# Modulation rows of a hybrid decoder layer: sums in two stages, products with ones at the stages' ends

## The chip, the cores and the metric

The kernel runs on one core of a Trainium2 chip. Times are device microseconds (us) of the whole program on that core. The profile shows one execution, with times counted from the start of its span.

## What is computed

One decoder layer for 1024 tokens of width 1024: a normalized and modulated input goes through one projection into four mixers (a forgetting attention, a chunked spatial gating, a Mamba-2 state space model, an mLSTM), whose outputs are normalized, joined and projected back; then a mixture of 32 experts, and a last norm. What the change touches is the modulation by the condition `c`:

```
cond = silu(c)
mod = cond @ w_ada + b_ada
shift1, scale1, gate1, shift2, scale2, gate2 = split(mod, 6)
h = rms_norm(x) * (1 + scale1) + shift1
x = x + gate1 * hybrid_mixer(h, ...)
h = rms_norm(x) * (1 + scale2) + shift2
x = x + gate2 * hierarchical_moe(h, ...)
```

`shift1` and `scale1` are made early. The other four rows of 1024 values (gate1, shift2, scale2 with the norm's gain folded in, gate2) are wanted only after the mixers, and go to a small table `mod_d` in device memory, one row each.

## The kernel before, in words

The program is a chain of stages, each written as a Python function. Data are tiles of 128 partitions. The mixers' input is held as a high and a low part (`hH`, `hL`), and so is each piece of weights (`wh`, `wl`): `load_w` loads `wraw` by SP (line 134; a second range by ACT), ACT writes the high part (line 53), DVE the low one (line 61), and every projection is three matmuls (hH wh, hH wl, hL wh) for each of eight slices of the inner dimension, in a PSUM bank named `ps`. Small products go to banks named `pq`.

Around the change the stages are, in the order of the program:

- the mLSTM's projections LQ, LK (channel-major, 128x512 matmuls), LV and LO (token-major: eight tiles of 24 matmuls of 128x256 each). ACT evicts them as `qT`, `kT`, `va` and, with a sigmoid, `so`. The eight `so` tiles are stored to `so_d` by SP (line 591) and loaded again as `ym` (line 658) when the outputs are made.
- the mLSTM's recurrence over eight chunks of 128 tokens (lines 597 to 649), then for each pair of chunks a head norm, the product with `ym` and a store to `y_tok` by SP (lines 650 to 660, 494).
- `ssd_inputs`: three pieces of projection; ACT evicts every bank twice, as `craw` and scaled as `xbc`; DVE adds the other three taps of a convolution, ACT applies SiLU. Then the state space model (`ssd`) and its output (`ssd_out`).
- `spatial_gating`: its weights `sgw` and gain `sgg` are loaded by ACT (lines 759, 765); eight tiles of `sgv`, two head norms, and eight tiles in which `ug` (ACT, two buffers) is multiplied into `sgy` (DVE, lines 782, 784), which SP stores.
- `attention_proj` (lines 791 to 823): 192 matmuls that give `q` and `k`, evicted by ACT and DVE; then the attention.

`modulation` (lines 546 to 565) is called ahead of the mLSTM. For each of the four rows it loads eight tiles `mw` of 512 KB by SP (three buffers), multiplies each by a column of `cond` and adds them up on DVE in `macc` (one buffer). Then ACT loads the row of `b_ada` into `mr` (one buffer), two matmuls of 512 columns with a column of ones sum `macc` over the partitions, DVE adds them to `mr`, and ACT stores the row to `mod_d`:

```
mr = mp.tile([1, 2, D], F32, name="mr", bufs=1)
nc.scalar.dma_start(mr[:, 0, :], b_ada[:, cs])
for c in (slice(0, 512), slice(512, D)):
    o = pq1()
    mm(o[0:1], ones[:, 0:1], acc[:, c], True, True)
    nc.vector.tensor_add(mr[:, 0, c], mr[:, 0, c], o[0:1])
nc.scalar.dma_start(mod_d[i:i + 1], mr[:, 0])
```

The order of each engine's instructions is not that of the text. A scheduler of the tile framework places them when the program is built, by its own estimate of when each could start; after that every engine, and every DMA queue (SP's, ACT's, POOL's), goes through its list in order. Tiles live in pools that open and close; a pool that opens in the memory of a closed one waits for the last instruction or transfer that used it.

Of the kernel before, what the change touches and what calls it, by code (L numbers as in the profile page):

```python
# [9 lines left out]
F32 = mybir.dt.float32  # L10
# [9 lines left out]
P = 128  # L20
S = 1024
D = 1024
# [14 lines left out]
def hybrid_block_kernel(ctx, tc, x, c, w_in, w_out, w_mix_norm, attn_f_bias, sg_w, sg_b,  # L37
# [4 lines left out]
    nc = tc.nc  # L42
# [12 lines left out]
    def mm(o, l, r, start, stop):  # L55
        return nc.tensor.matmul(o, l, r, start=start, stop=stop)  # L56
# [6 lines left out]
    def pool(stack, name, side, bufs=1):  # L63
        return stack.enter_context(tc.tile_pool(name=name, bufs=bufs, side=side))
# [7 lines left out]
    ones = consts.tile([P, P], F32, name="ones")  # L72
# [108 lines left out]
    with tc.tile_pool(name="st", bufs=1, side="left") as st, tc.tile_pool(name="stx", bufs=6, side="left") as stx, \  # L181
# [5 lines left out]
        xts, was, accs = {}, {}, {}  # L187
# [60 lines left out]
        for i in range(2):  # L248
            o = 0
# [29 lines left out]
        for g, (k0, k1) in enumerate(GS):  # L279
# [6 lines left out]
            acc = accs[g]  # L286
            o = pq1()
# [29 lines left out]
        for t in range(NT):  # L317
            o = os[t]
# [222 lines left out]

    tab_d = dram.tile([S * NE, 4], F32, name="tab_d")

    def modulation(mp):
        for i in range(4):
            cs = slice((2 + i) * D, (3 + i) * D)
            acc = mp.tile([P, D], F32, name="macc", bufs=1)
            for k in range(KT):
                wt = mp.tile([P, D], F32, name="mw", bufs=3)
                nc.sync.dma_start(wt, w_ada[k * P:(k + 1) * P, cs])  # L550
                if k == 0:
                    nc.vector.tensor_scalar(acc, wt, cond[:, k:k + 1], None, op0=OP.mult)
                else:
                    nc.vector.scalar_tensor_tensor(acc, wt, cond[:, k:k + 1], acc, op0=OP.mult, op1=OP.add)
            mr = mp.tile([1, 2, D], F32, name="mr", bufs=1)
            nc.scalar.dma_start(mr[:, 0, :], b_ada[:, cs])
            if i == 2:
                nc.scalar.dma_start(mr[:, 1, :], w_norm2)
            for c in (slice(0, 512), slice(512, D)):
                o = pq1()  # L560
                mm(o[0:1], ones[:, 0:1], acc[:, c], True, True)
                nc.vector.tensor_add(mr[:, 0, c], mr[:, 0, c], o[0:1])
            if i == 2:
                nc.vector.scalar_tensor_tensor(mr[:, 0], mr[:, 0], 1.0, mr[:, 1], op0=OP.add, op1=OP.mult)
            nc.scalar.dma_start(mod_d[i:i + 1], mr[:, 0])


    def mlstm(ml, wk):
# [17 lines left out]
        so_d = dram.tile([S, GW], F32, name="so_d")  # L586
        w = load_w((LO, LO + GW))
        for t in range(NT):
            so = wk.tile([P, GW], F32, name="so", tag="ym")
            act(so, tok_major(w, t)[:, :GW], AF.Sigmoid)  # L590
            nc.sync.dma_start(so_d[t * P:(t + 1) * P], so)

        C = [ml.tile([P, 2, 2 * VW], F32, name=f"C{i}") for i in range(2)]
        for i in range(2):
# [149 lines left out]
    def ssd_out(y, wk):  # L744
        w = load_w((MZ, MZ + GW))
        for t in range(NT):
            z = wk.tile([P, GW], F32, name="z")
            act(z, tok_major(w, t)[:, :GW], AF.Silu)
            nc.vector.tensor_mul(y[:, t, :], y[:, t, :], z)
        for t0 in (0, 4):  # L750
            yv = y[:, t0:t0 + 4, :].rearrange("p t (h d) -> p t h d", d=DH)
            head_norm(wk, yv, yv, 4)
            y_out(y[:, t0:t0 + 4, :], 2, t0, 4)
# [189 lines left out]
    ml = pool(m1, "ml", "right")  # L943
    mlw = pool(m1, "mlw", "right", 2)
    m2 = ExitStack()
    modulation(pool(m2, "mp", "right"))
    mlstm(ml, mlw)
    m2.close()
    m3 = ExitStack()
    xbc = ssd_inputs(pool(m3, "sA", "left"))  # L950
    m1.close()
    sB = pool(m3, "sB", "left", 2)
    y_ssd = ssd(xbc, sB)
    with ExitStack() as m4:
        ssd_out(y_ssd, sB)
        spatial_gating(pool(m4, "sgp", "right"))
    m3.close()
    with ExitStack() as m4:
        attention_proj(pool(ph1, "qp", "left"), pool(m4, "augp", "right"))
    proj.close()  # L960
# [176 lines left out]
    with ExitStack() as m4:  # L1137
# [263 lines left out]
        with tc.manual_schedule():  # L1401
# [15 lines left out]
            for t in range(NT):  # L1417
# [4 lines left out]
                o = ps1()  # L1422
                mixed(t, 0, o, 0, 4)
                if last:
                    x1T, f = turned(t - 1)
# [12 lines left out]
                if not last:  # L1438
# [3 lines left out]
                    f = [half(i) for i in range(2)]  # L1442
# [13 lines left out]
                o = ps1()  # L1456
# [761 lines left out]
```

## Time and profile before

| | us |
|---|---|
| median of 3 runs (lowest, highest) | 1273.74 (1273.19, 1274.29) |
| profiled execution | 1273.05 |
| its span | 1271.3 |
| mean granted clock of TensorE in it | 0.966 |
| PE busy | 1153.3 (91%) |
| DVE busy | 801.5 (63%) |
| ACT busy | 589.3 (46%) |
| POOL busy | 326.3 (26%) |

The profiled execution lies 1.75 us above its span, which counts from the first to the last instruction. In a timeline a row is one instruction (or several of a kind in a row, with their number): its start, its length, the engine, the source line, what it writes and reads; in brackets stand the idle time of the engine ahead of it and what ended it. A line 53, 56 or 61 is that of a helper, so the tiles' names tell which instruction it is. Issues of transfers on a queue carry a q behind the engine's name, and their length is that of the issue alone. A record of PE is longer than the distance to the next one, because matmuls are pipelined. The granted clock is a share of 2.4 GHz; 0.50 is 1.2 GHz.

### The profile page before, as it was taken

The page shows a single profiled execution, that of the slowest core. Times are in us where ns is not written, and L with a number is a line of the kernel's source. Part 1 is how long each engine was busy: PE and PEld are TensorE (multiplying, and loading weights), DVE is VectorE, ACT ScalarE, POOL GpSimd, SP SyncE. Part 2 cuts the span into 40 slices and gives each one's busy share as a digit, 9 for nine tenths or more (in the row PEclk, how much of TensorE's full clock was granted, in tenths as well). Part 3 has the DMA queues.
Part 4 walks back from the last instruction along what each step waited for, and adds up shares of the span by engine and source line. Part 5 has one row for each costly group of instructions (what it writes and reads, how often), then busy time and mean ns, then how long its engine had stood idle before and what let it go on. Part 6 is the DMA issues. An engine that isn't in the chain of part 4 may idle for free. (4 is left out here: it accounts for less than half of the span.)

```text
span 1271.3 us, 18583 instructions
## 1 busy us (share of the span) xinstructions
PE 1153.3 (91%) x6455; PEld 868.1 (68%) x6455; DVE 801.5 (63%) x1460; ACT 589.3 (46%) x909; POOL 326.3 (26%) x314
## 2 busy tenths in 40 slices
PE   4689879999999899999959999999999999999981
PEld 3577667879998788787747754466676557665660
DVE  6976667757643488488878941335654564555674
ACT  6442114354743488344437841224553443554563
POOL 2420000002102277333321942102322132222111
PEclk8699999999999999999969999999999999999996
DMA  9614884222221123675477999999999998999975
GB/s 268 203 32 149 261 271 118 89 71 53 73 60 34 42 65 111 203 267 199 162 296 290 328 332 377 376 403 372 385 378 378 357 389 317 341 367 384 337 274 198
DMA packets 96452, 305.48 MB, mean 240 GB/s; under 512 B 15106, under 2 KB 53756, under 8 KB 71772
## 3 DMA queue, kind: packets, MB, share of 16 engines
q1 hardware_dynamic: 84762, 284.47, 60.9%
q0 software_dynamic: 8464, 17.13, 5.8%
q10 hardware_dynamic: 3122, 2.56, 0.6%
q8 instruction: 57, 0.93, 0.3%
q14 instruction: 47, 0.39, 0.1%
HBM read 283.86 MB, written 32.06 MB: 249 GB/s over the span
## 5 line engine op out<-in xcount | busy, mean ns | idle before, releaser
L1649 POOL DMA_INDIRECT x_d<-yt,tabi x34 | 62.1, 1827 | 240.7 <-DVE yt L1623 186.7
L56 PE MATMUL ps<-wu,xTs 128*64 128x512 f32 x256 | 119.5, 599 | 1.8 <-DMA wu<-in_w_expert_up_dram 1.8
L56 PE MATMUL ps<-wg,xTs 128*64 128x512 f32 x256 | 119.8, 599 | 0.0
L56 PE MATMUL ps<-wh,hH 128*128 128x256 f32 (+1 forms) x336 | 96.9, 289 | 8.2 <-ACT so L53 4.9
L56 PE MATMUL ps<-wl,hH 128*128 128x256 f32 (+1 forms) x336 | 95.8, 286 | 0.0
L56 PE MATMUL ps<-wh,hL 128*128 128x256 f32 (+1 forms) x336 | 95.2, 288 | 0.0
L56 PE MATMUL ps<-hH,wh 128*128 128x512 f32 x224 | 89.1, 398 | 0.5 <-ACT xbc L53 0.4
L56 PE MATMUL ps<-hH,wl 128*128 128x512 f32 x224 | 89.4, 399 | 0.0
L56 PE MATMUL ps<-hL,wh 128*128 128x512 f32 x224 | 89.0, 397 | 0.0
L56 PEld LDWEIGHTS ps<-wh,hH 128*128 128x128 f32 x336 | 64.4, 192 | 11.4 <-ACT so L53 5.5
L56 PE MATMUL ps<-split,xTH 128*128 128x512 f32 x200 | 69.4, 403 | 1.0
L56 PEld LDWEIGHTS ps<-wg,xTs 128*64 128x64 f32 x256 | 32.1, 136 | 54.6 <-issue 51.3
L1640 POOL TENSOR_TENSOR yt<-yt,g2bc 128x1024 f32<-128x1024 f32 x14 | 33.7, 2409 | 137.5 <-ACT yt L53 121.4
L53 ACT ACT_TABLE_LOAD x47 | 60.3, 1283 | 17.7 <-DVE xbc L680 5.9
L53 ACT ACTIVATE xTH<-pq 128x512 fp32r<-128x512 f32 x33 | 18.4, 592 | 100.9 <-PE pq L1664 100.9
L56 PE MATMUL ps<-wh,xTH 128*128 128x512 f32 (+1 forms) x156 | 63.8, 409 | 1.4 <-PEq L1869 0.5
L56 PEld LDWEIGHTS ps<-wl,hH 128*128 128x128 f32 x336 | 64.1, 191 | 0.9 <-issue 0.9
L61 DVE TENSOR_TENSOR wl<-wu,wh 128x1024 fp32r<-128x1024 f32 x39 | 47.2, 1222 | 27.4 <-ACT wh L53 26.7
L56 PEld LDWEIGHTS ps<-wh,hL 128*128 128x128 f32 x336 | 64.3, 194 | 0.0
L56 PE MATMUL ps<-wl,xTH 128*128 128x512 f32 (+1 forms) x156 | 61.3, 393 | 0.5 <-DVE wl L61 0.5
L56 PE MATMUL pq<-wd,aTs 128*64 128x512 f32 x256 | 58.7, 597 | 3.0 <-PEq L1857 2.1
L53 ACT ACTIVATE sg<-ps 128x512 f32<-128x512 f32 (+1 forms) x32 | 18.9, 592 | 91.1 <-PE ps L56 49.8
(550 smaller groups left out, 3241.2 us busy)
## 6 DMA issues: line engine op xcount, KB each, us to landing
wg<-in_w_expert_gate_dram SPq DMA_DIRECT2D x64, 1024.0 KB, 9.5
wu<-in_w_expert_up_dram SPq DMA_DIRECT2D x64, 1024.0 KB, 8.1
wd<-in_w_expert_down_dram SPq DMA_DIRECT2D x64, 1024.0 KB, 7.5
mw<-in_w_ada_dram SPq DMA_DIRECT2D x32, 512.0 KB, 5.0
wraw<-in_w_in_dram SPq DMA_DIRECT2D x20, 512.0 KB, 3.6
xt<-in_x_dram SPq DMA_DIRECT2D x16, 512.0 KB, 4.1
wt<-in_w_ada_dram SPq DMA_DIRECT2D x16, 512.0 KB, 5.4
woraw<-in_w_out_dram SPq DMA_DIRECT2D x16, 256.0 KB, 3.4
```

The lines of the kernel that those rows point to most:

```text
L53: return nc.scalar.activation(o, i, f, **kw)
L56: return nc.tensor.matmul(o, l, r, start=start, stop=stop)
L61: (eng or nc.vector).tensor_sub(lo, src, hi.bitcast(F32))
L1640: nc.gpsimd.tensor_mul(yt[:, on_dve * 512:], yt[:, on_dve * 512:], g2bc[:, on_dve * 512:])
L1649: nc.gpsimd.indirect_dma_start(out=x1_d, out_offset=bass.IndirectOffsetOnAxis(ap=tok, axis=0), in_=yt, in_offset=None, bounds_check=S - 1, ...
```

## The change

`modulation` takes the rows `js` that it is to sum, keeps one `macc` tile for each, and returns a function that does the rest for these rows: `b_ada`'s load, the two products, the adds and the store. The rows 0 and 1 are summed beside the mLSTM's projections, and their products are written behind `mlstm`; the rows 2 and 3 are summed beside the gating, and their products are written behind `spatial_gating`. The `so_d` stores move from SP's queue to ACT's. `ssd_out` and the closing of its pools move ahead of the gating's pools. What is computed stays the same.

```diff
--- before.py
+++ after.py
@@ -541,10 +541,11 @@
 
     tab_d = dram.tile([S * NE, 4], F32, name="tab_d")
 
-    def modulation(mp):
-        for i in range(4):
+    def modulation(mp, js):
+
+        accs = {i: mp.tile([P, D], F32, name=f"macc{i}", bufs=1) for i in js}
+        for i, acc in accs.items():
             cs = slice((2 + i) * D, (3 + i) * D)
-            acc = mp.tile([P, D], F32, name="macc", bufs=1)
             for k in range(KT):
                 wt = mp.tile([P, D], F32, name="mw", bufs=3)
                 nc.sync.dma_start(wt, w_ada[k * P:(k + 1) * P, cs])
@@ -552,17 +553,26 @@
                     nc.vector.tensor_scalar(acc, wt, cond[:, k:k + 1], None, op0=OP.mult)
                 else:
                     nc.vector.scalar_tensor_tensor(acc, wt, cond[:, k:k + 1], acc, op0=OP.mult, op1=OP.add)
+
+        def rows_of(i):
+            cs = slice((2 + i) * D, (3 + i) * D)
             mr = mp.tile([1, 2, D], F32, name="mr", bufs=1)
             nc.scalar.dma_start(mr[:, 0, :], b_ada[:, cs])
             if i == 2:
                 nc.scalar.dma_start(mr[:, 1, :], w_norm2)
             for c in (slice(0, 512), slice(512, D)):
                 o = pq1()
-                mm(o[0:1], ones[:, 0:1], acc[:, c], True, True)
+                mm(o[0:1], ones[:, 0:1], accs[i][:, c], True, True)
                 nc.vector.tensor_add(mr[:, 0, c], mr[:, 0, c], o[0:1])
             if i == 2:
                 nc.vector.scalar_tensor_tensor(mr[:, 0], mr[:, 0], 1.0, mr[:, 1], op0=OP.add, op1=OP.mult)
             nc.scalar.dma_start(mod_d[i:i + 1], mr[:, 0])
+
+        def mod_rows():
+            for i in js:
+                rows_of(i)
+
+        return mod_rows
 
 
     def mlstm(ml, wk):
@@ -588,7 +598,7 @@
         for t in range(NT):
             so = wk.tile([P, GW], F32, name="so", tag="ym")
             act(so, tok_major(w, t)[:, :GW], AF.Sigmoid)
-            nc.sync.dma_start(so_d[t * P:(t + 1) * P], so)
+            nc.scalar.dma_start(so_d[t * P:(t + 1) * P], so)
 
         C = [ml.tile([P, 2, 2 * VW], F32, name=f"C{i}") for i in range(2)]
         for i in range(2):
@@ -943,18 +953,22 @@
     ml = pool(m1, "ml", "right")
     mlw = pool(m1, "mlw", "right", 2)
     m2 = ExitStack()
-    modulation(pool(m2, "mp", "right"))
+    mod_rows = modulation(pool(m2, "mp", "right"), (0, 1))
     mlstm(ml, mlw)
+    mod_rows()
     m2.close()
     m3 = ExitStack()
     xbc = ssd_inputs(pool(m3, "sA", "left"))
     m1.close()
     sB = pool(m3, "sB", "left", 2)
     y_ssd = ssd(xbc, sB)
+    ssd_out(y_ssd, sB)
+    m3.close()
     with ExitStack() as m4:
-        ssd_out(y_ssd, sB)
-        spatial_gating(pool(m4, "sgp", "right"))
-    m3.close()
+        sgp = pool(m4, "sgp", "right")
+        mod_rows = modulation(pool(m4, "mp", "right"), (2, 3))
+        spatial_gating(sgp)
+        mod_rows()
     with ExitStack() as m4:
         attention_proj(pool(ph1, "qp", "left"), pool(m4, "augp", "right"))
     proj.close()
```

What the scheduler makes of it, at three places. In the lists a row is a line of the program, an instruction and its tiles; xN stands for N in a row.

SP's queue beside the projections, before; `mw` are the sums' weights, `wraw` the projections' weights (the first here is LO's), `rb` rows that the recurrence reads:

```order
L550 DMA mw<-in_w_ada_dram 128x1024 x11
L134 DMA wraw<-in_w_in_dram 128x4x256
L550 DMA mw<-in_w_ada_dram 128x1024 x3
L134 DMA wraw<-in_w_in_dram 128x4x256
L550 DMA mw<-in_w_ada_dram 128x1024 x3
L599 DMA rb<-nrow_d 128x4x128
L550 DMA mw<-in_w_ada_dram 128x1024 x2
L599 DMA rb<-nrow_d 128x4x128
```

and after the change:

```order
L551 DMA mw<-in_w_ada_dram 128x1024 x16
L134 DMA wraw<-in_w_in_dram 128x4x256
L609 DMA rb<-nrow_d 128x4x128 x2
L134 DMA wraw<-in_w_in_dram 128x4x256
L609 DMA rb<-nrow_d 128x4x128 x2
L134 DMA wraw<-in_w_in_dram 128x4x256 x3
L668 DMA ym<-so_d 128x2x256
L134 DMA wraw<-in_w_in_dram 128x4x256
```

All 16 `mw` of the first two rows now stand ahead of LO's weights, where 11 of the 32 stood.

ACT at the end of the recurrence, before (`kt` and `ex` belong to the recurrence's last chunks, `hnq` and `hnv` to the head norms, `craw` and `xbc` are the first evictions of `ssd_inputs`):

```order
L53 ACTIVATE ex<-ex 128x512
L53 ACTIVATE hnq<-num 128x512
L53 ACTIVATE craw<-ps_2089 128x512
L53 ACTIVATE xbc_2085<-ps_2089,cols 128x512
L53 ACTIVATE kt<-pq_1882 128x256
L53 ACTIVATE kt<-pq_1925 128x256
L53 ACTIVATE ex<-ex 128x512
L53 ACTIVATE kt<-pq_1968 128x256
L53 ACTIVATE ex<-ex 128x512
L53 ACTIVATE hnq<-num 128x512
L53 ACT_TABLE_LOAD
```

and after the change, from the last `hnq` on:

```order
L53 ACTIVATE hnq<-num 128x512
L569 DMA mod_d<-mr 1x1024
L560 DMA mr<-in_b_ada_dram 1x1024
L53 ACTIVATE hnv<-hnv 128x8
L769 DMA sgw<-in_sg_w_dram 128x4x128
L569 DMA mod_d<-mr 1x1024
L775 DMA sgg<-in_w_mix_norm_dram 128x256
L53 ACTIVATE craw<-ps_2019 128x512
L53 ACTIVATE xbc_2015<-ps_2019,cols 128x512
L53 ACTIVATE craw<-ps_2046 128x512
L53 ACTIVATE xbc_2015<-ps_2046,cols 128x509
```

The two stores to `mod_d`, the load of `b_ada` between them and `sgw` now stand ahead of the first `craw` and `xbc`, which before stood between two `kt` of the recurrence. On PE the four products of rows 0 and 1 stand right behind the recurrence's last `va,ex`, three matmuls ahead of the end of a bank.

ACT at the end of the gating, before (`ug` are the gating's evictions, `q_0` and `k_0` the first of attention_proj):

```order
L53 ACTIVATE ug<-ps_3517 128x256
L53 ACTIVATE ug<-ps_3553 128x256
L53 ACTIVATE wh<-wraw 128x4x256
L134 DMA wraw<-in_w_in_dram 128x4x128
L53 ACTIVATE wh<-wraw 128x4x256
L53 ACTIVATE q_0_3609<-ps_3633 64x512
L53 ACTIVATE q_0_3610<-ps_3633 64x512
L53 ACTIVATE q_1_3621<-ps_3633 64x512
```

and after the change:

```order
L53 ACTIVATE ug<-ps_3538 128x256
L53 ACTIVATE wh<-wraw 128x4x256
L134 DMA wraw<-in_w_in_dram 128x4x128
L53 ACTIVATE wh<-wraw 128x4x256
L569 DMA mod_d<-mr 1x1024
L560 DMA mr<-in_b_ada_dram 1x1024
L569 DMA mod_d<-mr 1x1024
L53 ACTIVATE q_0_3613<-ps_3637 64x512
```

The stores of rows 2 and 3 and a load stand ahead of `q_0` and `k_0`. On PE the four products of rows 2 and 3 stand behind the gating's last `sgv,wT`, and the attention's first logits, which stood behind all 192 matmuls of attention_proj, stand behind its first 48.

## Rows read from the trace of the kernel before

**Rows 1.** The page, part 1: busy time (share) and instructions of each engine.

```profile
PE 1153.3 (91%) x6455; PEld 868.1 (68%) x6455; DVE 801.5 (63%) x1460; ACT 589.3 (46%) x909; POOL 326.3 (26%) x314
```

**Rows 2.** Busy time by stretch (us, instructions), granted clock, DMA share, GB/s.

```profile
160.00:200.00 40.00, 31.53 (x233) 27.14 (x234) 23.07 (x31) 7.39 (x14) 0.00 (x0) 1.00 0.67 227
200.00:250.00 50.00, 49.62 (x337) 40.15 (x338) 43.43 (x126) 24.53 (x41) 3.12 (x5) 1.00 0.34 96
...
350.00:400.00 50.00, 50.00 (x389) 48.26 (x389) 20.05 (x30) 17.39 (x28) 1.90 (x2) 1.00 0.20 56
```

**Rows 3.** Waits of PE, 100 to 200 us: total us, times, longest.

```profile
PE ps L56 <- ACT so L53: 4.9, 3, 3.0
PE pq L56 <- DVE macc L554: 4.5, 2, 2.9
...
PE ps L56 <- ACT va L53: 0.7, 1, 0.7
```

**Rows 4.** Timeline of PE beside the projections: start, length, instruction, idle time before it.

```profile
128.94 0.39 PE L56 MATMUL ps<-hH,wh 128*128 128x512 f32 x1
129.17 0.40 PE L56 MATMUL ps<-hH,wl 128*128 128x512 f32 x1
131.96 3.27 PE L56 MATMUL pq<-macc,ones 128*1 128x512 f32 x4 [2.39 <-issue]
...
137.12 0.28 PE L56 MATMUL ps<-wh,hH 128*128 128x256 f32 x1
137.24 0.28 PE L56 MATMUL ps<-wl,hH 128*128 128x256 f32 x1
...
171.43 1.88 PE L56 MATMUL pq<-macc,ones 128*1 128x512 f32 x4 [2.94 <-DVE macc L554]
...
199.88 0.72 PE L56 MATMUL pq<-qT,kT 64*128 64x128 f32 x8
```

**Rows 5.** Timeline of SP's DMA issues, 110 to 250 us.

```profile
112.06 20.15 SPq L550 DMA_DIRECT2D mw<-in_w_ada_dram  x11
132.26 0.43 SPq L134 DMA_DIRECT2D wraw<-in_w_in_dram  x1
...
239.96 0.36 SPq L658 DMA_DIRECT2D ym<-so_d  x1
```

**Rows 6.** Groups of DVE instructions, 110 to 200 us: busy and mean, idle before.

```profile
L554 DVE SCALAR_TENSOR_TENSOR macc<-mw,cond,macc 128x1024 f32<-128x1024 f32 x28 | 36.4, 1301 | 13.2 <-DMA mw<-in_w_ada_dram 12.8
...
L562 DVE TENSOR_TENSOR mr<-mr,pq 1x512 f32<-1x512 f32 x8 | 5.4, 674 | 5.4 <-PE pq L56 5.4
...
L671 DVE MEMSET craw<- 128x3 f32 x1 | 0.1, 61 | 1.3 <-DMA mod_d<-mr 1.3
```

**Rows 7.** Timeline of ACT, 112 to 400 us.

```profile
138.88 1.06 ACT L53 ACTIVATE wh<-wraw 128x1024 fp32r<-128x1024 f32 x1 [0.96 <-DMA wraw<-in_w_in_dram]
...
154.27 0.22 ACTq L565 DMA_DIRECT2D mod_d<-mr  x1
...
160.48 0.22 ACTq L556 DMA_DIRECT2D mr<-in_b_ada_dram  x1
...
219.13 0.58 ACT L53 ACTIVATE craw<-ps 128x512 f32<-128x512 f32 x1
...
396.75 1.06 ACT L53 ACTIVATE wh<-wraw 128x1024 fp32r<-128x1024 f32 x1 [5.38 <-DMA wraw<-in_w_in_dram]
```

**Rows 8.** Timeline of PE: end of the recurrence, and of the gating.

```profile
233.96 0.47 PE L56 MATMUL ps<-hH,wh 128*128 128x512 f32 x1
...
390.65 0.48 PE L56 MATMUL ps<-hH,wh 128*128 128x512 f32 x1
```

**Rows 9.** DMA issues, 108 to 200 us: KB each, median us to landing.

```profile
ym<-so_d SPq DMA_DIRECT2D x1, 256.0 KB, 2.8
```

**Rows 10.** Busy time by stretch (as rows 2), first logits of the attention.

```profile
440.00:445.00 5.00, 4.21 (x20) 3.63 (x20) 2.46 (x7) 2.72 (x9) 4.18 (x4) 0.50 0.15 57
```

**Rows 11.** Timeline of DVE, 250 to 256 us.

```profile
253.81 0.35 DVE L700 SCALAR_TENSOR_TENSOR ex<-rb,cum,mneg 128x128 f32<-128x128 f32 x1 [2.74 <-DMA rb<-arow_d]
```

## The prediction

> **What bounds the kernel now.** I read the page's totals first, then the busy time by stretch, then the waits of PE, then the timelines of PE, ACT, DVE and SP around the two places where the change puts its products. The totals say that PE works 91% of the span and DVE 63% [rows 1], so what counts is where PE still stands idle. The stretches say where: from 160 to 200 us, beside the mLSTM's projections, PE is busy 31.5 of 40 us, while the recurrence behind it (200 to 250) and the gating (350 to 400) run at 49.6 and 50.0 of 50 [rows 2]. So one stage has air in it, and the stages that the change loads further have none. The waits between 100 and 200 us are 4.9 for ACT's `so`, 4.5 for DVE's `macc` and 0.7 for `va` [rows 3], and 2.4 in front of the first products at 131.96 [rows 4]: 12.5 us. The `so` waits come from `so_d` stores that stand behind `mw` loads on SP; most of the others from products that sit in the middle of PE's order and wait for DVE's sums.
>
> **The sum is made against the profiled run's 1273.05 us; the median of the runs is 0.69 higher. About 2.5 us (0.2%) is what a measurement can tell from no change.**
>
> **Part A: the projections lose the products.** Without them LK ends at about 131.0: its last matmul before the wait stands at 129.17, the pitch is 0.23 (128.94 to 129.17) [rows 4], and seven more follow. LV and LO are 16 token tiles of 24 matmuls at a pitch of 0.118 (137.12, 137.24) [rows 4], 2.83 us each, 45.3 in all, so PE could end at 176.3 instead of 199.88, where the recurrence's first logits stand now [rows 4]. But SP now issues 16 `mw` in a row ahead of LO's first `wraw`. Eleven took 20.15 us [rows 5], 1.98 each, paced by three buffers and DVE's 1.30 us sums [rows 6], so the sixteenth goes out near 141.8 and `wraw` near 142.2. In the run before, such a `wraw`, issued at 132.26 behind `mw` [rows 5], had ACT waiting until 138.88 [rows 7], 6.6 us. So LO's first weights land near 148.8; ACT splits them in 1.06 [rows 7] and only then evicts the fourth `va`, which stands behind that split in ACT's order. PE wants that bank for LV's sixth tile at 131.0 + 5 x 2.83 = 145.2 and gets it near 150.2: a new wait of 5.0. I add 0.8 for the second half of the weights. The moved `so_d` stores leave SP, and the 4.9 us go. LO ends near 182.1: **-17.8 us** (-19.5 if `wraw` is quicker, -13 if it waits out another three loads and the clock falls after the wait).
>
> The recurrence itself is PE-dense before and after, and shifts as a block.
>
> **Part B: the end of the recurrence.** Times here are those of before, where the last va,ex product gives way at 233.96 [rows 8].
> - Each row has two products, and two of the four rows now stand here. One row's two took 1.88 (171.43) [rows 4]; two rows are 3.8 by the records, and I take 3.4, since records on PE overlap (those of 0.40 start 0.23 apart). A has lost all eight products, so these four are added here: **+3.4**.
> - ACT's order at this place now runs: store row 0, load `b_ada` for row 1 (one `mr` buffer, so it waits until the store has landed), `sgw`, store row 1, and only then the evictions of `craw` and `xbc`. In the run before, the first of these evictions was done at 219.13, in the recurrence [rows 7]. Now they also wait for row 1's landed store, because the pool `sA` takes the memory of the closed pool of the sums. `sgw` takes memory of the mLSTM's tiles and waits for the last `ym` product. That chain: the `ym` load went out at 239.96 [rows 5]; row 0's two adds, 0.67 each [rows 6], hold DVE back 1.4 more, 241.4; the load takes 2.8 [rows 9], 244.2; the `ym` product and row 1's last add, by the same 0.67, 245.5; the store lands 1.3 later by what DVE's `craw` memset waited for it [rows 6], 246.8; two evictions of 0.58 [rows 7], 248.0. PE has only the last three matmuls of a bank before it needs one of these: 233.96 + 3.4 + 0.7 = 238.1. **+10 us** of new idle (8 if `ym` comes sooner, 12.5 if the store meets the `sgw` load).
> - Behind a wait the clock falls: after attention_proj, where PE waits for the first logits, the granted clock is 0.50 in 440 to 445, the lower level of 1.2 GHz [rows 10]; and behind the 2.4 us wait one row's products took 3.27 instead of 1.88 [rows 4], a loss of 1.4. By the first row the loss is half of 5 us or more, by the second 1.4. I take **+2.5**, nearer to the first, since this wait is the longer one (1.4 to 3.4).
> - The first SiLU stands in DVE's order behind `ex<-rb`, which waited 2.7 us for its load, until 253.81 [rows 11], while PE had other banks to fill. The load goes out behind the `ym` stores, later by about 1.4, and PE's cover is used up: **+2** (0 to 4).
>
> **Part C: the gating.** DVE gets 16 sums, some 20 us at 1.30 [rows 6], into a stretch where it is busy 20 of 50 us [rows 2]: room enough in total, but its order puts the first `sgy` products behind the ninth to sixteenth sums, which come at the pace of the loads (1.98). `ug` has two buffers, so the third `ug` eviction waits for the first `sgy` product, and PE for its bank. A tile of the gating has 24 matmuls too, 2.83 us, and its products; I take one tile's time, **+3** (0.5 if the loads are quicker, 6 if two tiles are late). Four products: **+3.4**. Then ACT has row 2's store, `b_ada` and row 3's store ahead of the first `q` eviction, which again waits for the landed store. ACT ends its second `wh` at 397.8 [rows 7]; store 1.3, load 2.8, adds 1.3, store 1.3: 404.5; four evictions at 0.58 and one DVE add: 407.5. The first attention logits now stand after 48 of attention_proj's matmuls, so PE needs them at 390.65 [rows 8] + 3.4 + 48 x 0.23 = 405.1: **+2.4** (0 to 5).
>
> **Sum:** -17.8 + (3.4 + 10 + 2.5 + 2) + (3 + 3.4 + 2.4) = **+8.9 us**, 1281.95 us, call it **1282**. Behind attention_proj I see no term: what reads `mod_d` comes after it. With every bound at its good end it is -19.5 + (3.4 + 8 + 1.4) + (0.5 + 3.4) = -2.8, with every bound at its bad end -13 + (3.4 + 12.5 + 3.4 + 4) + (6 + 3.4 + 5) = +24.7; the ends don't all meet, so this case's own range is 1276 to 1290.
>
> **A rule weighed.** A `mod_d` store of 4 KB took 1.3 us when nothing else was in flight [rows 6], but under the `mw` stream the next `b_ada` load, which waits for it, went out only 6.2 us after it (154.27, 160.48) [rows 7]. I price it at 1.3, as the `mw` stream has ended in both places. The Trainium skill ("DMA: Bandwidth & Descriptors", Latency and other measured facts) says that the memory's access latency is 0.2 us on average and 2 us at high load, and that lighter load makes a DMA's fixed cost smaller. The trace agrees in direction, 1.3 against 6.2. It bears on the third rival below, where the stores do meet other loads.
>
> **The rivals.**
> 1. *Faster: the eviction isn't held.* ACT is through with its chain soon after PE needs the bank: the last `ym` load goes out earlier, since its `so_d` rows were stored long before. Then B is the 3.4 of products alone: -17.8 + 3.4 + 8.8 = -5.6, **1267.4** (1265 if the sums cost C only 0.5). It decides at 17.8 - 3.4 - 8.8 = 5.6 us of stall with its after-effects: below that the change wins. Against it: SP issues that load at 239.96 [rows 5] behind the `y_tok` stores whose buffer it takes, 6 us after the last va,ex, and they end the same head norms as before. Chance 0.22.
> 2. *No change: B is about half.* The stall is 5 with no clock loss and no later waits: -17.8 + 8.4 + 8.8 = -0.6, **1272.5**. Chance 0.12.
> 3. *Slower still: the stores meet loads.* `sgw` and `rb` at the first place, `wraw` at the second are in flight beside the four critical stores. If two of these cost 4 more each (between 1.3 and 6.2), +8 comes on top: **1290**. No row shows a store beside `sgw`, and its 256 KB are little against the `mw` stream. Chance 0.16. By the Trainium skill's rule above, loaded stores would do just this.
> 4. The forecast: chance 0.50.
>
> That the products really leave the projections is seen in PE's order, so a change that does nothing is no case.
>
> **The numbers.** Faster by over 0.2% is rival 1, 0.22; within 0.2% rival 2, 0.12; slower the forecast and rival 3, 0.66. The range for 8 in 10 takes in most of rival 1 and of rival 3: **1265 to 1292**.
>
> **What would show it.** In the profile after: the recurrence's first logits near 182, not 199.9; no product between 112 and 182; one PE wait of about 5 on `va` or ACT's `wh`. Some 3 us behind the last va,ex, a PE wait of 8 to 12 us that ends on ACT's `xbc`, itself released by a `mod_d` store; behind it a stretch at the lower clock. In the gating, waits on `ug` or `sgy` of 3 us together, and a wait of 2 to 3 on `q` or `k` where the first logits stand. The forecast is wrong if ACT's first `craw` comes within 5 us of the last va,ex, or if LO ends later than 187.

## The result, and the profile after

The changed kernel takes **1289.28 us** (median of 4 runs, 1286.09 to 1290.57), the kernel before 1273.93 on the same chip (1273.19 to 1274.29): ratio 1.0108, 95% interval 1.0093 to 1.0123, or 12 to 16 us slower. The profiled execution took 1288.98, 15.9 more than the profiled 1273.05 of before, where +8.9 had been forecast. Direction and range hold; the size was nearly twice the forecast.

The totals of the page (part 1, as [rows 1]):

```profile
PE 1158.6 (90%) x6455; PEld 874.8 (68%) x6455; DVE 799.8 (62%) x1460; ACT 589.4 (46%) x909; POOL 324.7 (25%) x314
```

The same 6455 instructions keep PE busy 5.3 us longer, and the span is 15.8 longer. So a third of the loss is PE working more slowly, the rest is PE idle. The busy time by stretch (columns as [rows 2]) says where:

```profile
160.00:200.00 40.00, 40.00 (x331) 36.71 (x329) 17.23 (x48) 15.19 (x26) 1.87 (x3) 1.00 0.42 115
200.00:250.00 50.00, 39.28 (x221) 29.42 (x220) 34.24 (x100) 18.26 (x30) 1.25 (x2) 0.90 0.26 72
350.00:400.00 50.00, 45.48 (x347) 41.81 (x346) 37.03 (x46) 14.97 (x23) 0.00 (x0) 0.97 0.65 209
```

From 160 to 200 PE is now full, 40.00 of 40 where it had 31.53 [rows 2]. The air has moved: 200 to 250 fell from 49.62 to 39.28 with the clock at 0.90, and 350 to 400 from 50.00 to 45.48 at 0.97. The waits of PE between 100 and 460 us (total us, times, longest) name what ends its idle times:

```profile
PE ps L56 <- ACT xbc L53: 10.7, 1, 10.7
PE ps L56 <- ACT va L53: 5.3, 1, 5.3
PE ps L56 <- ACT ug L53: 4.1, 1, 4.1
PE pq L56 <- DVE mx L851: 3.7, 4, 1.4
PE ps L56 <- DVE q L824: 1.5, 1, 1.5
PE pq L56 <- ACT k L53: 1.3, 1, 1.3
```

The `so` and `macc` waits of [rows 3] are gone. In their place stand `va`, `xbc`, `ug`, `q` and `k`; the `mx` waits were there before (3.5).

PE's timeline in four places (start, length, instruction; in brackets the idle time ahead of it), first the end of the projections, then the end of the recurrence, the gating, and the first logits of the attention:

```profile
183.50 0.71 PE L56 MATMUL pq<-qT,kT 64*128 64x128 f32 x8
...
217.76 3.59 PE L56 MATMUL pq<-macc,ones 128*1 128x512 f32 x8
221.28 0.50 PE L56 MATMUL ps<-hH,wh 128*128 128x512 f32 x1
...
221.85 0.40 PE L56 MATMUL ps<-hL,wh 128*128 128x512 f32 x1
232.97 0.79 PE L56 MATMUL ps<-hH,wh 128*128 128x512 f32 x1 [10.72 <-ACT xbc L53]
...
379.41 0.58 PE L56 MATMUL ps<-wh,hH 128*128 128x256 f32 x1 [4.12 <-ACT ug L53]
...
395.95 3.59 PE L56 MATMUL pq<-macc,ones 128*1 128x512 f32 x8
399.48 0.50 PE L56 MATMUL ps<-hH,wh 128*128 128x512 f32 x1
...
412.14 0.33 PE L56 MATMUL pq<-k,q 128*128 128x128 f32 x1 [1.28 <-ACT k L53]
...
414.07 0.77 PE L56 MATMUL ps<-hH,wh 128*128 128x512 f32 x1 [1.52 <-DVE q L824]
```

Read it as a balance, profiled execution against profiled execution, at instructions that stand in both kernels:

| up to | before | after | after - before | this stretch |
|---|---|---|---|---|
| the recurrence's first logits | 199.88 | 183.50 | -16.4 | -16.4 |
| its last `va,ex` | 233.93 | 217.56 | -16.4 | 0 |
| the state space model's first matmul | 291.58 | 289.96 | -1.6 | +14.8 |
| the gating's first transpose of `sgw` | 337.66 | 336.18 | -1.5 | +0.1 |
| the gating's last `sgv,wT` | 390.62 | 395.75 | +5.1 | +6.6 |
| attention_proj's first matmul | 390.65 | 399.48 | +8.8 | +3.7 |
| attention_proj's last matmul | 434.99 | 450.04 | +15.1 | +6.2 |
| the attention's last `pl,vh` | 511.26 | 527.76 | +16.5 | +1.5 |
| end of the span | 1271.3 | 1287.1 | +15.8 | -0.7 |

The change wins 16.4 us where it takes products out. It gives back 14.8 at the end of the recurrence, and another 16.5 from the gating to the end of attention_proj. What the attention's 1.5 are worth is taken up below.

The long wait, on ACT's side (timeline of ACT at the end of the recurrence):

```profile
220.38 0.24 ACTq L569 DMA_DIRECT2D mod_d<-mr  x1
221.68 0.25 ACTq L560 DMA_DIRECT2D mr<-in_b_ada_dram  x1
...
228.40 0.41 ACTq L769 DMA_DIRECT2D sgw<-in_sg_w_dram  x1
228.93 0.33 ACTq L569 DMA_DIRECT2D mod_d<-mr  x1
...
231.75 0.60 ACT L53 ACTIVATE craw<-ps 128x512 f32<-128x512 f32 x1 [7.71 <-DMA mod_d<-mr]
232.24 0.68 ACT L53 ACTIVATE xbc<-ps,cols 128x512 f32<-128x512 f32 x1
```

The bank that PE wants back is ready from about 222. ACT stands idle, because ahead of the first `craw` its list has `sgw`'s load, which goes out at 228.40, and row 1's store, at 228.93; and `craw` itself begins only when that store has landed, at 231.75. So the store took 2.8, where an earlier one had been seen at 1.3 [rows 6]. It goes out so late because DVE adds row 1's second half behind the last `ym` product, which waits for its load (timeline of DVE):

```profile
227.53 0.69 DVE L669 TENSOR_TENSOR ym<-ym,num 128x512 f32<-128x512 f32 x1 [1.94 <-DMA ym<-so_d]
228.14 0.67 DVE L566 TENSOR_TENSOR mr<-mr,pq 1x512 f32<-1x512 f32 x1
```

The other two places are of the same make (timelines of DVE and ACT):

```profile
372.57 1.28 DVE L555 SCALAR_TENSOR_TENSOR macc<-mw,cond,macc 128x1024 f32<-128x1024 f32 x1 [2.56 <-DMA mw<-in_w_ada_dram]
...
378.44 0.41 DVE L794 TENSOR_TENSOR sgy<-sgy,ug 128x256 f32<-128x256 f32 x1
...
378.97 0.38 ACT L53 ACTIVATE ug<-ps 128x256 f32<-128x256 f32 x1 [6.56 <-DVE sgy L794]
...
407.34 1.07 ACT L53 ACTIVATE q<-ps 64x512 fp32r<-64x512 f32 x2 [4.37 <-DMA mod_d<-mr]
```

The third `ug` waits for the first `sgy` product, which stands on DVE behind three sums and two steps of the head norm; the first `q` waits for row 3's store.

What follows a wait is slow too. Busy time by stretch (as [rows 2]) around the three places where PE stood, the end of the recurrence, attention_proj, and the attention's first chunk:

```profile
225.00:230.00 5.00, 0.00 (x0) 0.00 (x0) 1.86 (x4) 0.00 (x0) 0.00 (x0) 0.56 0.38 99
230.00:235.00 5.00, 2.03 (x5) 1.64 (x6) 1.25 (x8) 2.24 (x4) 0.00 (x0) 0.50 0.50 127
235.00:240.00 5.00, 5.00 (x22) 4.01 (x21) 3.53 (x8) 0.15 (x1) 0.00 (x0) 0.92 0.24 68
...
410.00:415.00 5.00, 2.19 (x8) 1.47 (x7) 2.40 (x4) 3.33 (x6) 0.30 (x1) 0.83 0.01 3
415.00:420.00 5.00, 5.00 (x13) 3.89 (x12) 1.05 (x2) 0.00 (x0) 2.54 (x3) 0.50 0.01 2
...
460.00:465.00 5.00, 5.00 (x25) 3.93 (x25) 3.26 (x7) 3.27 (x7) 4.89 (x5) 0.55 0.16 52
```

PE counts as fully busy from 415 to 420 and still does 13 matmuls where 23 fit into five microseconds at full clock (x23 from 400 to 405): that loss never shows as a wait. In the kernel before, the place of the program that the last row shows comes 15 us earlier:

```profile
445.00:450.00 5.00, 5.00 (x42) 4.05 (x42) 4.41 (x9) 3.99 (x9) 4.92 (x5) 0.87 0.18 56
```

### The profile page after: what moved, and what is told of

The parts are those of the page before. It is cut to its first block, busy times and chain, and to the rows that moved or that the text cites. A ratio compares the mean times of both kernels' runs of the same rounds, so it can differ in the third digit from the quotient of the medians.

```text
span 1287.1 us, 18587 instructions
## 1 busy us (share of the span) xinstructions
PE 1158.6 (90%) x6455; PEld 874.8 (68%) x6455; DVE 799.8 (62%) x1460; ACT 589.4 (46%) x909; POOL 324.7 (25%) x314
## 5 line engine op out<-in xcount | busy, mean ns | idle before, releaser
L56 PE MATMUL ps<-hH,wh 128*128 128x512 f32 x224 | 91.1, 407 | 12.2 <-ACT xbc L53 10.7
L56 PEld LDWEIGHTS ps<-wh,hH 128*128 128x128 f32 x336 | 65.5, 195 | 14.3 <-ACT va L53 5.5
L56 PE MATMUL ps<-wh,xTL 128*128 128x512 f32 (+1 forms) x156 | 60.6, 389 | 0.1
```

## The experiments

The theory behind the runs: two mechanisms, each a wait on memory that is used again. At the recurrence's end, `sA` opens in memory of the closed pool of the sums, so ACT's first eviction waits until row 1's store has landed. In the gating, `ug` has two buffers, whose reader `sgy` stands in DVE's order behind sums that wait for `mw` loads. The rivals: it is ACT's queue that holds its own work back (a matter of order, not memory); it is the products or the split as such; or the moved `so_d` stores. Each run's ratio is to the kernel before on the same chip, where that kernel's median was 1276.5 to 1276.8. The changed kernel was measured where it was 1273.93, so runs are compared with the changed kernel by the ratios (1.0108 for that one) and by the profiles, not by the times alone.

**1. Stores and loads of the rows on another queue.** All DMAs of the rows go from ACT to POOL.

```diff
-            nc.scalar.dma_start(mr[:, 0, :], b_ada[:, cs])
+            nc.gpsimd.dma_start(mr[:, 0, :], b_ada[:, cs])
...
-            nc.scalar.dma_start(mod_d[i:i + 1], mr[:, 0])
+            nc.gpsimd.dma_start(mod_d[i:i + 1], mr[:, 0])
```

> The changed kernel with the loads of b_ada and the stores to mod_d issued by POOL in place of ACT; nothing else. Theory (the evictions of craw and xbc wait because the pool sA takes the memory of mr, so that row 1's store must have landed): the wait stays, PE stands 8 to 12 us for xbc at the end of the recurrence, and the time is 1283 to 1294 us. Rival (ACT's own queue holds them, since its stores and loads stand ahead of them in its order): with the transfers off ACT that wait falls under 5 us, and the time is 1272 to 1281 us.

Measured: 1291.07, ratio 1.012 (1.0079 to 1.0161), and the `xbc` wait of PE is 11.8, not shorter. ACT's waits between 200 and 250 us:

```profile
ACT craw L53 <- DMA mod_d<-mr: 8.8, 1, 8.8
```

ACT has no store of a row on its queue any more, and `craw`, which reads nothing of a row, still waits for one. So the wait goes with the store to POOL's queue, and what the two share is the memory. ACT's order isn't out of it, though: `sgw`'s load still stands ahead of `craw` and goes out at 229.43 only, ACT is through with its issues at 230.4, and `craw` begins at 233.91. Of the wait the store alone holds the last 3.5 us.

**2. Rows 0 and 1 without their late load and store.** They leave `b_ada` out (the adds become copies) and are written as ones at the program's start.

```diff
+            if i > 1:
-            nc.scalar.dma_start(mod_d[i:i + 1], mr[:, 0])
+                nc.scalar.dma_start(mod_d[i:i + 1], mr[:, 0])
...
+    nc.scalar.dma_start(mod_d[0:2].rearrange("a (b c) -> (a b) c", c=P), ones[:16, :])
```

> The changed kernel without b_ada's load and the store for rows 0 and 1 (these two rows are set to ones by an early store; products and adds stay, written as copies). Theory: with no store to wait for, the wait for xbc falls from 10.7 us to under 3, and the time is 9 to 13 us below the changed kernel's 1289, 1276 to 1280. Rival (the wait is that for the last ym product, or for the products with ones themselves): it stays at 6 us or more, and the time is 1284 to 1290 us.

Measured: 1500.2, a time that can't be compared, because rows 0 and 1 (`gate1`, `shift2`) now hold other values: what stands behind the attention takes 978 us instead of 759. That other experts get the tokens would explain it and was not looked into. The stretch can be read: the `xbc` wait is 3.9 instead of 10.7, and from the last `va,ex` to the state space model's first matmul it takes 65.8 instead of 72.4. So load and store account for 6.8 of the 10.7; some 3.9 remain, a little more than expected. There `craw` begins when DVE's last copy of row 1 is done (timeline of ACT):

```profile
227.86 0.60 ACT L53 ACTIVATE craw<-ps 128x512 f32<-128x512 f32 x1 [0.39 <-DVE mr L570]
```

So the rest too is a wait on the row's memory, and the products as such are not what holds the place. `sgw` went out behind `craw` here, at 232.18; the order of ACT changed with the store.

**3. All four rows' sums first, products behind the mLSTM.**

```diff
-        for i in range(4):
+        accs = {i: mp.tile([P, D], F32, name=f"macc{i}", bufs=1) for i in range(4)}
+        for i, acc in accs.items():
...
     mlstm(ml, mlw)
+    mod_rows()
```

> The kernel before with only the products moved: all four rows summed beside the projections, all eight products, adds and stores behind mlstm; b_ada's rows and the norm's gain take buffers of mw, so_d stores stay on SP. No sums in the gating. Theory: the chain of stores and loads at the end of the recurrence is now four rows long, so PE's wait for xbc is 15 to 25 us, the eight products take 7 us there, the gating loses nothing, and the projections gain less than 16 us; 1280 to 1295 us. Rival (splitting the sums over two stages is what costs, through the gating): under 1276 us.

Measured: 1303.36, ratio 1.0216 (1.0169 to 1.0263), and neither the time nor the `xbc` wait (8.6) is as expected. The longest wait is a different one, between 90 and 470 us:

```profile
PE ps L56 <- ACT wh L53: 28.6, 2, 28.4
PE ps L56 <- ACT xbc L53: 8.6, 1, 8.6
```

With 32 `mw` in one row ahead of LO's weights on SP's queue, PE waits 28.4 us for these weights; the changed kernel's 16 cost 5.3 (`va`). That is the price of part A's own mechanism: in this order of loads it is far dearer with four rows than with two. From the last `va,ex` to the state space model's first matmul it takes 77.6, where the kernel before takes 57.7; why the `xbc` wait is no longer than 8.6 with four rows in the chain stays open.

**4. The split, but the products right behind their sums.** `mod_rows()` is called ahead of `mlstm` and ahead of `spatial_gating`.

```diff
-    mlstm(ml, mlw)
     mod_rows()
+    mlstm(ml, mlw)
...
-        spatial_gating(sgp)
         mod_rows()
+        spatial_gating(sgp)
```

> The changed kernel with each half's products written right behind its sums, so beside the projections and beside the gating, not at the stages' ends. Theory: no wait for xbc at the end of the recurrence and none for q at the start of attention_proj, since the stores have landed long before; the projections gain about 9 us against the kernel before in place of 16, the gating still loses 6 to 12 us by its sums and four products; 1270 to 1282 us. Rival (the products cost the same wherever they stand, since PE is the bound): 1285 us or more.

Measured: 1280.66, ratio 1.0043 (1.0022 to 1.0064). The first logits stand at 186.08 and the state space model begins at 277.19, 14.4 ahead of before: 13.8 of part A's 16.4 come without moving the products, from two rows' sums instead of four and the moved `so_d` stores; 9 had been expected. There is no long `xbc` wait. Moving the products to the recurrence's end wins 2.6 more (183.50) and costs 15.3 (72.4 from the last `va,ex` to the state space model's first matmul, 57.1 here). In the gating the products in place lose more than the late ones: a wait on `macc` of 9.9 at the longest, and the last `sgv,wT` at 395.42, 4.8 behind the kernel before, so 19.2 lost, four products among it, where 6 to 12 had been expected and the changed kernel loses 6.7 from the same point on, and 3.7 more by the products behind it. The time lies in the expected range because two misses offset each other.

**5. The moved `so_d` stores alone**, in the kernel before.

```diff
-            nc.sync.dma_start(so_d[t * P:(t + 1) * P], so)
+            nc.scalar.dma_start(so_d[t * P:(t + 1) * P], so)
```

> The kernel before with only the so_d stores moved from SP's queue to ACT's; products and sums as before. Theory: the 4.9 us that PE waits for so, and little else, go, so the time falls by 2 to 6 us. Rival (the products in PE's order take up the time anyway, or the stores delay ACT's evictions): within 2 us of the kernel before.

Measured: 1274.35, ratio 0.9979 (0.9959 to 1.0): at most a trace of a gain. The `so` wait falls from 4.9 to 0.3, but `macc` grows from 4.5 to 6.9, and the first logits stand at 200.54 instead of 199.88. The products in PE's order take up what the stores gave free. What the stores are worth together with the split was not tried by itself.

**6. Six `ug` buffers in the gating's pool.**

```diff
-            ug = sg.tile([P, GW], F32, name="ug", bufs=2)
+            ug = sg.tile([P, GW], F32, name="ug", bufs=6)
```

> The changed kernel with six buffers for ug in place of two; nothing else. Theory (the third ug eviction waits for a buffer that DVE frees only behind the sums, and PE for its bank): the wait for ug in the gating (4.1 us) and the lower clock behind it go, and the time is 3 to 7 us below the changed kernel's 1289. Rival (PE then waits at the same place for a pq bank, which DVE's sgy frees behind the same sums): the wait only changes its name, and the time stays within 2 us.

Measured: 1298.9, ratio 1.0177 (1.0147 to 1.0206), some 9 us slower than the changed kernel, which neither expectation had. The `ug` wait is down to 1.5, but ahead of the gating stands a new one (timelines of ACT and PE):

```profile
345.44 0.40 ACTq L769 DMA_DIRECT2D sgw<-in_sg_w_dram  x1
...
354.37 1.09 PE L772 MATMUL pq<-ident,sgw 128*128 128x128 f32 x4 [12.72 <-DMA sgg<-in_w_mix_norm_dram]
```

The larger pool reaches into memory that the state space model still uses, so ACT issues the load of `sgw` at 345.44, beside the first `mw` loads, where the changed kernel does so at 228.40. Run 10 bears this out: with as many buffers in another pool `sgw` goes out at 228.44. It is the same kind of wait as at the recurrence's end, brought on by 4 KB more per partition.

**7. The products turned, and the rows kept as columns.** `macc` becomes the stationary operand and a column of ones moves; the result is a 128x8 tile in a pool that stays open. Biases are loaded at the start, SP stores.

```diff
-                mm(o[0:1], ones[:, 0:1], accs[i][:, c], True, True)
+            for k in range(KT):
+                mm(o[:, k:k + 1], accs[i][:, k * P:(k + 1) * P], ones[:, 0:1], True, True)
...
-            nc.scalar.dma_start(mod_d[i:i + 1], mr[:, 0])
+            nc.sync.dma_start(mod_d[i].rearrange("(k p) -> p k", p=P), mc)
```

> The changed kernel with the products turned round: macc is the weights, a column of ones is streamed, eight products of one column for a row instead of two of 512; biases and the norm's gain come with the other vectors at the start, the row's result is a tile of 128x8 in a pool that stays open, and SP stores it. So no load and no store of ACT stands at a stage's end, and sA's memory has no store to wait for. Theory: the wait for xbc at the end of the recurrence falls from 10.7 us to under 3, the four products at either end from 3.5 us to under 1.5, the wait at the start of attention_proj goes; 15 to 22 us below the changed kernel, 1267 to 1274 us. Rival (the end of the recurrence is bound by the head norms and ym's last load in any case): the wait for xbc stays over 6 us, 1278 us or more.

Measured: 1282.56, ratio 1.0048 (1.0012 to 1.0084), 8.6 above the upper end of what was expected. The `xbc` waits shrink to 4.2 in all, as the theory wants, but two prices were wrong. The sixteen products (groups of PE, out<-in and count, then busy time and mean ns; each product shows as two matmuls) are no cheaper than the four of the changed kernel (x8), which took 3.59:

```profile
L56 PE MATMUL pq<-ones,macc 128*128 128x1 f32 x32 | 3.6, 247 | 0.0
```

And the stores are now 1024 pieces of 4 bytes each: at the recurrence's end two of them went out at 215.54 and 217.33, and the second landed 11.0 us after its issue. At the gating's end what is issued behind them comes late (timelines of SP and ACT):

```profile
388.30 1.41 SPq L570 DMA_DIRECT2D mod_d<-mcols  x2
390.50 0.37 SPq L136 DMA_DIRECT2D wraw<-in_w_in_dram  x1
...
403.80 1.06 ACT L53 ACTIVATE wh<-wraw 128x1024 fp32r<-128x1024 f32 x1 [17.70 <-DMA wraw<-in_w_in_dram]
```

The weights issued at 390.50 are there at 403.80, after 13.3 us. In the kernel before the same load took 4.1: it is used at 396.75 [rows 7] and was issued at 392.66 (timeline of SP):

```profile
392.66 0.38 SPq L134 DMA_DIRECT2D wraw<-in_w_in_dram  x1
```

PE waits 6.9 for `q` because of it. That the stores are the reason is the likeliest reading; they were not tried apart from the rest of this run.

**8. Run 7 with six `ug`, and eight `mw` in the second half.**

```diff
-                wt = mp.tile([P, D], F32, name="mw", bufs=3)
+                wt = mp.tile([P, D], F32, name="mw", bufs=3 if js[0] == 0 else 8)
...
-            ug = sg.tile([P, GW], F32, name="ug", bufs=2)
+            ug = sg.tile([P, GW], F32, name="ug", bufs=6)
```

> The kernel columns with six buffers for ug and, for the second half, eight for mw. Theory: beside what columns gives, the gating's waits go too; 3 to 7 us below columns, 1261 to 1270 us, below the kernel before. Rival (a pq bank or DVE's order holds PE in the gating): no better than columns by 2 us.

Measured: 1295.97, ratio 1.0154 (1.0122 to 1.0185), a miss for the reason of run 6: `sgw`'s load goes out at 335.14, where run 7 issues it at 233.39, and PE's transposes of `sgw` wait 14.3 us. No `ug` wait is left; the gain there is lost ahead of it.

**9. Rows 0 and 1 in memory that is not taken.** The rows are written in the tile `qT` of the mLSTM, free at that point and outliving the opening of `sA`; both `b_ada` loads go out at the recurrence's end.

```diff
-            mr = mp.tile([1, 2, D], F32, name="mr", bufs=1)
+            mr = old[0:1, i:i + 1, :] if old is not None else mp.tile([1, 2, D], F32, name="mr", bufs=1)
...
-    mlstm(ml, mlw)
-    mod_rows()
+    mod_rows(mlstm(ml, mlw))
```

> The changed kernel with rows 0 and 1 written in qT, a tile of the mLSTM that is dead behind the recurrence and whose pool outlives ssd_inputs' opening; both loads of b_ada go out at the recurrence's end, and no store or load lies in memory that sA takes. In the built order the first craw and xbc then stand ahead of row 1's store on ACT, and SP has LO's weights ahead of the last ten mw. Theory: the wait for xbc falls from 10.7 us to under 3, the gating and the start of attention_proj stay as they are; 10 to 16 us below the changed kernel's 1289, 1273 to 1279 us, of which 3 to 5 by the earlier weights. Rival (ym's last load or the products hold the place in any case): the wait stays at 6 us or more and the time is 1283 us or more.

Measured: 1275.64, ratio 0.9996 (0.9981 to 1.0011), as expected. The `xbc` waits are 2.3 in all, and the state space model begins at 276.47, 15.1 ahead of before. The same products stand in the same place on PE; the edit touches only the memory and the times of the loads. With these ACT's order changed: the first `craw` and `xbc` now stand ahead of row 1's store and of `sgw`. Together with runs 1 and 2 that shows the first mechanism, a wait on the row's memory that also sets ACT's order (the two weren't taken apart), and its price: from the last `va,ex` to the state space model's first matmul it takes 62.9 us instead of 72.4 (57.7 in the kernel before), 9.5 less. Another 4.0 come from ahead of it: the first logits stand at 179.47 instead of 183.50. The scheduler laid the early work differently too: the sixteen `mw` go out from 80.0 to 111.9 instead of from 112.1 on, all ahead of LO's first weights (119.6, and not ten behind them as expected). The `va` wait of 5.3 is gone, and two waits on `pre` (3.2 in all) are new. Why it did so was not looked into. What the change loses behind it, in the gating and attention_proj, remains and uses up the whole gain.

**10. Six `ug` in the pool of the sums**, where they push nothing.

```diff
-            ug = sg.tile([P, GW], F32, name="ug", bufs=2)
+            ug = up.tile([P, GW], F32, name="ug", bufs=6)
...
+        mp = pool(m4, "mp", "right")
+        mod_rows = modulation(mp, (2, 3))
+        spatial_gating(sgp, mp)
```

> The changed kernel with six buffers for ug, taken from the pool of the sums in place of the gating's own, so that sgw and sgg stay clear of the memory of the state space model's tiles (in ug_six they were moved into it). Theory: the wait for ug of 4.1 us and the lower clock behind it go, without ug_six's wait for sgw; 3 to 7 us below the changed kernel, 1282 to 1286 us. Rival (PE then waits for a pq bank that sgy frees behind the same sums): within 2 us of the changed kernel.

Measured: 1285.11, ratio 1.0068 (1.0043 to 1.0092), as expected. No `ug` wait is left, and the last `sgv,wT` stands at 391.13, 4.6 earlier than in the changed kernel. Counted from the state space model's first matmul it takes 99.6 to there, where the changed kernel takes 105.8 and the kernel before 99.0: the second mechanism, with what follows its wait, costs 6.2 of the 6.7 lost. A wait of 3.1 on `aug` in the attention is new, and the `xbc` wait is 10.7 as in the changed kernel.

**11. Both mended**: runs 9 and 10, and a `mr` tile for each of rows 2 and 3, so that the second load waits for no store.

```diff
+            mr = old[0:1, i:i + 1, :] if old is not None else mp.tile([1, 4 - i, D], F32, name=f"mr{i}", bufs=1)
...
+            ug = up.tile([P, GW], F32, name="ug", bufs=6)
...
+    mod_rows(mlstm(ml, mlw))
```

> rows_in_qT and ug_in_mp together, and two mr tiles for rows 2 and 3 whose loads go out early in the gating, so that only two stores stand ahead of q. Theory: the waits for xbc, ug and q go or fall under 2 us each, and what stays of the change is its gain at the projections less the eight products' 7 us at the stages' ends: 17 to 24 us below the changed kernel, 1265 to 1272 us, below the kernel before by 2 to 9. Rival (the sums, not the waits, are what the gating pays): 1275 us or more.

Measured: **1269.18** (1268.86 to 1270.67), ratio 0.9939 (0.9917 to 0.9961): faster than both kernels. PE's waits between 90 and 470 us, the first lines:

```profile
PE pq L56 <- DVE mx L852: 3.8, 4, 1.2
PE ps L56 <- ACT xbc L53: 2.3, 2, 1.9
PE ps L56 <- DVE q L825: 2.1, 1, 2.1
PE pq L56 <- DVE pre L370: 2.0, 1, 2.0
```

And PE and ACT at the recurrence's end (timelines):

```profile
215.74 3.59 PE L56 MATMUL pq<-macc,ones 128*1 128x512 f32 x8
...
220.60 0.50 PE L56 MATMUL ps<-hH,wh 128*128 128x512 f32 x1 [0.36 <-ACT xbc L53]
...
219.37 0.60 ACT L53 ACTIVATE craw<-ps 128x512 f32<-128x512 f32 x1 [1.51 <-PE pq L56]
...
222.89 0.23 ACTq L569 DMA_DIRECT2D mod_d<-qT  x1
```

Row 1's store now goes out at 222.89, behind the first eviction at 219.37, and nothing waits for it; the wait that was 10.72 is 0.36. The first logits stand at 181.47 and the last `sgv,wT` at 379.45, where before had 199.88 and 390.62: of the 18.4 won in the projections, 11.2 are left at the end of the gating. attention_proj then takes another 6, the products (3.5) and `q` (2.1) nearly all of it, and 5.1 are left at its end (429.85 against 434.99). Of the lead over the changed kernel 2.0 stand at the first logits already, with the early loads laid as in run 9 (the first `mw` at 81.2).

## Why the prediction was right in direction and short in size

- **Part A, right.** Forecast -17.8, measured -16.4. The new wait is there as worked out, on `va`, 5.3 for a forecast 5.0, and LO ends 1.4 later than forecast (183.5 for 182.1). Run 4 adds that the shorter sums and the moved stores bring most of it (13.8), not the departure of the products.
- **Part B, the wait right, its tail too dear.** 17.9 was forecast for the stretch, and 14.8 measured. Products 3.5 for 3.4; the wait 10.7 for 10, by the chain that was worked out (`ym`, row 1's add, its store, eviction). Runs 1, 2 and 9 show that the wait is one on memory. The store's landing took 2.8 instead of 1.3, with `sgw`'s load issued 0.5 us ahead of it; that the load is the reason was not tried by itself, and with one such store it is a small piece of rival 3, not its 8 us. The clock is at 0.50 from 230 to 235, as forecast, but it holds for six matmuls alone, with steps of 0.59 once and then 0.43 instead of 0.33 and 0.23, which makes 1.3, not 2.5. That is one execution: in run 10 fourteen matmuls are slow behind the same wait of 10.7, some 2.9 us, so 2.5 was no bad price. And the 2 for a late SiLU wait did not come: the stretch is even 0.7 shorter than products, wait and clock together.
- **Part C, the step that failed.** 3 was put down for the sums and 2.4 for attention_proj beside 3.4 of products, 8.8 in all; measured were 6.6 and 6.2 beside 3.7, 16.5. The waits themselves were nearly right: `ug` 4.1, and `k` and `q` together 2.8. What the sum left out is the slow stretch behind each of them, priced once in part B and not here. Behind `ug` there are thirteen steps of 0.21 from matmul to matmul (379.79 to 382.56) instead of 0.12, 1.2 us, and a wait of 0.4 on `sgv`, ahead of it, was not foreseen either; run 10 shows that `ug` with what follows it is nearly the whole loss of the gating. Behind `q` the steps of fourteen matmuls are 0.43 instead of 0.23, 2.8 us, where the clock is 0.50 from 415 to 420 (in runs 1, 2 and 6 only seven matmuls are slow behind the same two waits, some 1.4 us, so half of the 2.8 belongs to this one execution). In the kernel before, this stretch of attention_proj ran at full clock, with its logits behind all matmuls.
- **"Behind attention_proj I see no term": not shown to be wrong.** The profiles differ by 1.5 there. In the attention's first chunk the waits are those of before, but the clock stays low for one stretch longer: 0.55 with 25 matmuls from 460 to 465. In the kernel before the five microseconds at the same place of the program (445 to 450) have 0.87 and 42. That alone is (0.87 - 0.55) x 5 = 1.6. But run 5, which changes nothing from the recurrence on, has it too: its stretch from the end of attention_proj to the last `pl,vh` is 77.5 long, where before has 76.3 and the changed kernel 77.7. The 1.5 are nothing that the change is shown to cost.
- **The bounds.** The errors partly cancel: part A brought 1.4 less and part C cost 7.7 more than forecast, while part B cost 3.1 less, and the rest makes about 1. So the size is nearer than its terms are, and that is luck. +15.9 lies inside the case's +24.7 at the bad ends, and inside the range; the two terms off most were the ones for which no row showed the place itself. Rival 1 fell with the wait: its deciding point was 5.6 us of stall, and 10.7 came. Runs 9 and 11 make that rival's condition true. By itself it gives no change, since part C costs more than the rival assumed (run 9); with the `ug` wait gone as well it gives a faster kernel (run 11).

## What to carry to other kernels

When work is moved to the end of a stage, ask whose memory it holds there: a next stage's pool waits for the last reader of what it covers, a small store too. Another queue did not help (run 1), memory that nobody takes did (run 9). A larger pool can do the same to loads that went out early (run 6), so put added buffers where nothing is waiting to open. And price every wait of TensorE twice, its idle time and the slow stretch behind it: here the waits of the gating and attention_proj cost 6.9, and the stretches behind them another 4 in the profiled execution. That second price is a range, not a figure: between the runs it differed by half for the same waits.

## What the runs showed of the hardware

- How many matmuls run at the lower level (granted clock 0.50) behind a wait did not follow from the wait. Behind 10.7 us without a matmul it was six in the changed kernel and fourteen in run 10; behind two waits of 1.3 and 1.5, close together, fourteen in the changed kernel, thirteen in run 9, and seven in runs 1, 2 and 6; behind a single one of 2.1 none (run 11, steps of 0.23 throughout).
- Four products of 512 columns with one column as weights (eight matmuls in the profile) and sixteen products of one column with 128 columns as weights (32 matmuls) take the same 3.6 us: 0.45 and 0.11 a matmul. Turning a thin product gains nothing here.
- A store of 1024 pieces of 4 bytes is issued in 0.4 us of SP's time, like any other (the 1.41 of run 7's row are two, with a pause between them), but it landed 11.0 us after its issue at the recurrence's end, behind another one, where a row in one piece took 1.3 to 2.8. The 256 KB pieces of weights issued right behind two of them took 13.3 us to be there instead of 4.1 (run 7). The stores were not tried apart from the rest of that run.
